# Attention scores of both half heads issued as pairs, with a softmax by chunks of keys

## The chip, the cores and the metric

The kernel runs on one core of a Trainium2 chip. Its time is the device time in microseconds (us) of one execution, as the median of several runs. The engines are named as in the profile: PE multiplies matrices (PEld loads its weights), DVE and ACT work on vectors, POOL adds and issues gathers, SP issues the other transfers.

## What is computed

The reference is one layer of a diffusion backbone over 1024 latent tokens and 256 context tokens of width 1024: modulated norm, one input projection, retention beside differential attention, an output projection with a gated residual, then an expert retrieval (PEER) with another gated residual. The change touches only the attention:

```python
def diff_softmax_attend(q, k, v, lam):
    s = jnp.einsum('bhpqd,bhpkd->bhpqk', q, k).astype(jnp.float32) * (DIFF_D ** -0.5)
    p = jax.nn.softmax(s, axis=-1)
    a = (p[:, :, 0] - lam * p[:, :, 1]).astype(v.dtype)
    return jnp.einsum('bhqk,bhke->bhqe', a, v)
```

There are 4 heads, each of two half heads (index p) of 64 columns. Each half has its own softmax over 1280 keys (1024 latent, 256 context); the second, times lambda, is subtracted from the first. In the expert retrieval each token picks 16 of 16384 experts for each of 8 retrieval heads by two short lists of 128 keys, and sums their outputs.

## The kernel before, in words

**The stages.** Tokens go in 8 blocks of 128. First come the projections of all tokens and the retention. Then `mix` runs over the groups of blocks [0], [4, 5], [6, 7], [3], [1, 2]: `attend` for each block of a group, then the output projection and the norm. `route` follows for each group: query projections, the short lists (`top16`) and the `select` of the experts, on DVE. Blocks 0 to 2 are served by gathers of expert rows (768 of them, each 128 rows of 1024 numbers): POOL issues one, DVE forms a product (`gat<-gat,h2t`) or adds one up (`acc<-gat,act,acc`). Blocks 3 to 7 are served by a dense phase over all experts on PE; ahead of it `gates` writes their weights as a table (`t<-iota`, `o<-iota` on DVE, `o<-o,pt` on ACT). The dense phase needs the gates of block 3, the last; beside its first matmuls the selects of blocks 1 and 2 are still on DVE. The gathers go on beside the dense phase.

**One head of `attend`** (lines 1078 to 1117). For each half p it issues three score matmuls (`mm<-k,t`: 512, 512 and 256 keys) over the 64 partitions of the half, three maxima on DVE, the maximum of the three and its scaling (`m<-m`), then three exponentials on ACT with their sums. When both halves are there, DVE forms the factor `rs`; ACT scales the second half by it (`h<-h,rs`, `u<-u,rs`), and DVE (odd heads) or POOL (even heads, `EC`) adds it to the first (`h<-h`, `u<-u,u`). PE transposes the result in blocks of 128 (`mm<-ident,h`), ACT copies it out, and PE multiplies it with the values (`mm<-v,aT`, `mm<-v,u`).

**What sets the order.** Every operation is recorded and put in order by a planner (class `Plan`): a list scheduler with one queue an engine, modelled costs, priorities, and buffers as limited resources (PSUM is the tag `mm`, 8 banks). `weave` spreads the recorded parts over spans of a common priority (`QSPAN`, `ASPAN`, `HSPAN` and so on), `HOLD` keeps gathers back for a stretch, `PACES` sets their rhythm. Operations inside `with nc.unit()` stay together. Each engine then works through its own list in order. All instructions are issued from one line, so the profile shows line 563 for all; they are told apart by tile names.

Of the kernel before, what the change touches and what calls it, by code (L numbers as in the profile page):

```python
# [30 lines left out]
HOLD = [1000, 1600]  # L31
# [6 lines left out]
QSPAN = [[-0.2, 0.475], [0.1, 1], [-0.05, 1.309], [-0.35, 1.05], [0.15, 0.9]]  # L38
# [3 lines left out]
LSPAN = [[0.479, 1.05], [0.565, 1.218], [0.436, 1.3], [0.05, 0.85]]  # L42
G2SPAN = [0.182, 0.991]
VL, CL, EC, XE = 'D', 'D', 'PD', 'PPPPPPPP'
POFF, PACES = 40, [[0, 3.6], [200, 3.0], [300, 1.17], [700, 1.18], [1100, 1.9]]
# [8 lines left out]
HSPAN = [[-0.25, 0.85], [0.05, 0.796], [0.2, 1.538]]  # L54
# [92 lines left out]
class Plan:  # L147
# [118 lines left out]
    def cost(self, eng, meth, a, k, outs, vs):  # L266
# [303 lines left out]
def layer(tc, I, out, dbg=None):  # L570
# [3 lines left out]
    with sp as S, pp as P, dp as DR:  # L574
        bufs = {"mm": 8, "h": 8, "k": 5, "rv": 4, "b": 4, "v": 5, "sel": 3, "wst": 4, "gat": 4, "fin": 2,  "u1": 3, "u2": 2, "u3": 2,
                "o": 1, "vi": 2, "egb": 3, "pt": 2, "m4": 4, "s1": 2, "act": 2,  "gsum": 2, "rs": 2, "ssum": 2}
# [15 lines left out]
        def ps(shape):  # L592
            return nc.tile(shape, F32, "mm")
# [288 lines left out]
        def qk(kb, pm, which, h0):  # L882
# [185 lines left out]
        def attend(b, res):  # L1068
# [9 lines left out]
            for h in range(H):  # L1078
                nm = sb([128, 2, 4], "m4")
                ssum = sb([128, 2, 4], "ssum")  # L1080
                pl, pc = [], []
                for p in range(2):
                    r = slice(p * 64, (p + 1) * 64)
                    sc3 = [ps([128, 512]), ps([128, 512]), ps([128, 256])]
                    rhs = [KTl[h][r, 0:512], KTl[h][r, 512:1024], KTc[r, h, :]]
                    for i in range(3):
                        nc.tensor.matmul(sc3[i], QT[r, h, :], rhs[i], start=True, stop=True)
                        nc.vector.reduce_max(out=nm[:, p, i:i + 1], in_=sc3[i], axis=AX.X)
                    nc.vector.reduce_max(out=nm[:, p, 3:4], in_=nm[:, p, 0:3], axis=AX.X)
                    nc.vector.tensor_scalar(nm[:, p, 3:4], nm[:, p, 3:4], -SC, None, op0=OP.mult)  # L1090
                    el = sb([128, SEQ], "h")
                    ec = sb([128, CTX], "u1")
                    dsts = [el[:, 0:512], el[:, 512:1024], ec]
                    for i in range(3):
                        nc.scalar.activation(dsts[i], sc3[i], AF.Exp, scale=SC, bias=nm[:, p, 3:4],
                                             accum_out=ssum[:, p, i:i + 1])
                    pl.append(el)
                    pc.append(ec)
# [479 lines left out]
```

## Time and profile before

| | |
|---|---|
| median of 3 runs | 3464.39 us (3459.51 to 3482.91) |
| the profiled execution | 3468.12 us, its span 3466.0 us |
| busy, share of the span | PE 92%, DVE 79%, ACT 38%, POOL 34% |
| mean granted clock of PE | 0.961 of 2.4 GHz |

Busy shares over the whole span hide the stages. The dense phase begins at about 1580 us; attention lies between 400 and 1400 us. So the profile is read by stretches. A group row names an engine, an operation, what it writes and reads, the shape, the count, then busy time, the mean of one in ns, and the idle time of the engine just before with what ended it. A matmul of 4-byte numbers stands as two instructions, so 128 of 512 columns show as x256.

### The profile page before, as it was taken

How to read it: one execution, taken by the hardware profiler on the slowest of the kernel's cores; microseconds unless marked ns; L12 is line 12 of the kernel's file. 1: busy time of each engine (PE TensorE's matmuls, PEld its weight loads, DVE VectorE, ACT ScalarE, POOL GpSimd, SP SyncE). 2: the span in 40 equal slices, each digit the busy share in tenths (PEclk: the TensorE clock that was granted, in tenths of full speed). 3: DMA queues.
4: the chain of work that ended last, by engine and by line, in shares of the span. 5: the costliest groups of instructions: out<-in, count | busy, mean ns of one | idle time of the engine just before them, and what ended most of it. 6: DMA issues, size and time to landing. Idle time of an engine off the chain costs nothing. (4 is left out here: it accounts for less than half of the span.)

```text
span 3466.0 us, 51310 instructions
## 1 busy us (share of the span) xinstructions
PE 3200.0 (92%) x18240; PEld 2745.9 (79%) x18240; DVE 2724.9 (79%) x5902; ACT 1315.0 (38%) x3466; POOL 1188.9 (34%) x1051
## 2 busy tenths in 40 slices
PE   7999996879889789896999999999999999999998
PEld 4998575556678667785898888888889888888887
DVE  4456447779898977969787888788878887888788
ACT  4342343424348679872332222222222222222221
POOL 0101121554340201201454445354545443445442
PEclk9999998889999789997999999999999999999999
DMA  5222655776574434553888888888888888888886
GB/s 183 98 80 83 195 201 172 247 280 232 170 250 163 168 134 141 183 198 113 298 293 298 292 300 282 273 290 301 289 289 297 300 291 271 289 295 292 289 294 231
DMA packets 314529, 809.67 MB, mean 234 GB/s; under 512 B 29313, under 2 KB 125593, under 8 KB 314274
## 3 DMA queue, kind: packets, MB, share of 16 engines
q1 hardware_dynamic: 203682, 403.70, 34.7%
q0 software_dynamic: 110592, 402.70, 33.9%
q8 instruction: 144, 2.36, 0.3%
q14 instruction: 111, 0.91, 0.1%
HBM read 745.46 MB, written 60.83 MB: 233 GB/s over the span
## 5 line engine op out<-in xcount | busy, mean ns | idle before, releaser
L563 PE MATMUL mm<-k,h 128*128 128x384 f32 (+1 forms) x4096 | 916.7, 310 | 20.7 <-DVE h L563 13.3
L563 PEld LDWEIGHTS mm<-k,h 128*128 128x128 f32 x4096 | 693.2, 188 | 35.1 <-DVE h L563 14.9
L563 POOL DMA_INDIRECT gat<-peer_v,egb x377 | 498.1, 1321 | 598.7 <-DVE acc L563 425.2
L563 PE MATMUL mm<-v,h 128*128 128x384 f32 (+1 forms) x2048 | 629.5, 307 | 0.0
L563 ACT CAST h<-wst 128x512 fp32r<-128x512 f32 (+1 forms) x384 | 287.9, 763 | 873.1 <-PE mm L563 841.6
L563 PE MATMUL mm<-h,rv 128*128 128x512 f32 x2304 | 594.8, 397 | 23.8 <-DVE rv L563 22.5
L563 POOL DMA_INDIRECT gat<-peer_u,egb x360 | 421.5, 1171 | 547.8 <-DVE gat L563 287.5
L563 PEld LDWEIGHTS mm<-h,rv 128*128 128x128 f32 x2304 | 425.7, 189 | 127.1 <-DVE rv L563 30.5
L563 DVE SCALAR_TENSOR_TENSOR acc<-gat,act,acc 128x1024 f32<-128x1024 f32 x375 | 480.4, 1281 | 46.2 <-DMA gat<-peer_v,egb 44.7
L563 DVE SCALAR_TENSOR_TENSOR gat<-gat,h2t 128x1024 f32<-128x1024 f32 x360 | 450.8, 1255 | 52.6 <-DMA gat<-peer_u,egb 52.1
L563 PE MATMUL mm<-h,t 128*128 128x512 f32 (+1 forms) x1600 | 423.0, 394 | 15.4 <-DVE b L563 8.3
L563 DVE TENSOR_TENSOR h<-wst,h 128x512 fp32r<-128x512 f32 (+1 forms) x384 | 328.8, 867 | 134.7 <-issue 102.8
L563 PEld LDWEIGHTS mm<-v,h 128*128 128x128 f32 x2048 | 385.1, 188 | 6.3
L563 PEld LDWEIGHTS mm<-h,t 128*128 128x128 f32 x1600 | 295.2, 190 | 88.9 <-DVE b L563 13.6
L563 PE MATMUL mm<-b,wst 128*128 128x256 f32 (+1 forms) x1280 | 242.1, 346 | 3.3 <-ACT b L563 1.5
L563 POOL TENSOR_TENSOR m<-m,mhalf 128x4 f32<-128x4 f32 (+1 forms) x78 | 74.5, 958 | 479.8 <-DVE m L563 469.7
L563 PEld LDWEIGHTS mm<-b,wst 128*128 128x128 f32 x1280 | 208.7, 197 | 30.1 <-issue 3.5
L563 DVE TENSOR_TENSOR b<-b,mm 128x512 f32<-128x512 f32 x248 | 166.3, 684 | 77.6 <-PE mm L563 77.0
L563 PE MATMUL mm<-t,h 128*128 128x256 f32 x992 | 186.8, 286 | 5.9 <-DVE aT L563 3.5
L563 ACT CAST rv<-aT 128x384 fp32r<-128x384 f32 x128 | 65.8, 514 | 329.1 <-DVE aT L563 315.9
L563 DVE TENSOR_TENSOR t<-iota,pt 128x512 f32<-128x512 f32 x240 | 177.2, 772 | 13.3 <-PE mm L563 13.2
L563 PE MATMUL mm<-k,t 64*128 64x512 f32 (+1 forms) x384 | 167.4, 584 | 13.3 <-ACT h L563 12.7
(234 smaller groups left out, 4876.1 us busy)
## 6 DMA issues: line engine op xcount, KB each, us to landing
wst<-peer_u_cols SPq DMA_DIRECT2D x128, 512.0 KB
wst<-peer_v_halves SPq DMA_DIRECT2D x128, 512.0 KB
wst<-w_query_chunks SPq DMA_DIRECT2D x80, 512.0 KB
h<-Wd SPq DMA_DIRECT2D x64, 512.0 KB
wst<-w_mod_chunks SPq DMA_DIRECT2D x48, 512.0 KB
wst<-w_out_chunks SPq DMA_DIRECT2D x40, 512.0 KB
Wd<-rv SPq DMA_DIRECT2D x40, 512.0 KB
Wd<-gat SPq DMA_DIRECT2D x40, 512.0 KB
```

What stands on the lines that cost most here:

```text
L563: getattr(handles[n.eng], meth)(*[res(v) for v in a], **k)
```

## The change

`attend` issues the scores by chunks of keys: for each chunk the two matmuls of both halves stand in one unit, next to each other. Each chunk takes its own maximum on DVE (negated at once) and its exponential follows with that maximum; the scale of 1/8 now lies in the query's copy. When all six chunks are there, factors `f`, the exponentials of the differences between the row's maximum and the chunks' maxima, bring sums and values to the row's maximum. ACT scales each chunk of the second half by its factor; one multiply-add on DVE (`scalar_tensor_tensor`) scales the chunk of the first half and adds. `EC` is 'D' now: DVE does this for all heads and POOL for none. The planner's cost of a matmul over 64 partitions with 256 columns or more is halved, and some numbers of its table differ.

```diff
-HOLD = [1000, 1600]
+HOLD = [1000, 1550]
...
-QSPAN = [[-0.2, 0.475], [0.1, 1], [-0.05, 1.309], [-0.35, 1.05], [0.15, 0.9]]
+QSPAN = [[0.1, 0.475], [0.1, 1], [-0.05, 1.309], [-0.35, 1.05], [0.15, 0.9]]
...
-LSPAN = [[0.479, 1.05], [0.565, 1.218], [0.436, 1.3], [0.05, 0.85]]
+LSPAN = [[0.479, 1.05], [0.565, 1.218], [0.436, 1.3], [0.2, 0.85]]
...
-VL, CL, EC, XE = 'D', 'D', 'PD', 'PPPPPPPP'
-POFF, PACES = 40, [[0, 3.6], [200, 3.0], [300, 1.17], [700, 1.18], [1100, 1.9]]
+VL, CL, EC, XE = 'D', 'D', 'D', 'PPPPPPPP'
+POFF, PACES = 40, [[0, 3.6], [200, 3.0], [300, 1.17], [700, 1.06], [1100, 1.9]]
...
-HSPAN = [[-0.25, 0.85], [0.05, 0.796], [0.2, 1.538]]
+HSPAN = [[-0.25, 0.8], [0.05, 0.796], [0.2, 1.838]]
...
-            return 4 * max(n, 64) * (0.4 if outs[0].shape[0] == 32 else 1) / 2330.0, 0, None, False
+            return 4 * max(n, 64) * (0.5 if n >= 256 and a[1].shape[0] == 64 else 1) / 2330.0, 0, None, False
...
-                nc.scalar.copy(qs, tp)
+                nc.scalar.activation(qs, tp, AF.Copy, scale=SC)
...
-                pl, pc = [], []
-                for p in range(2):
-                    r = slice(p * 64, (p + 1) * 64)
-                    sc3 = [ps([128, 512]), ps([128, 512]), ps([128, 256])]
-                    rhs = [KTl[h][r, 0:512], KTl[h][r, 512:1024], KTc[r, h, :]]
-                    for i in range(3):
-                        nc.tensor.matmul(sc3[i], QT[r, h, :], rhs[i], start=True, stop=True)
-                        nc.vector.reduce_max(out=nm[:, p, i:i + 1], in_=sc3[i], axis=AX.X)
-                    nc.vector.reduce_max(out=nm[:, p, 3:4], in_=nm[:, p, 0:3], axis=AX.X)
-                    nc.vector.tensor_scalar(nm[:, p, 3:4], nm[:, p, 3:4], -SC, None, op0=OP.mult)
...
-                        nc.scalar.activation(dsts[i], sc3[i], AF.Exp, scale=SC, bias=nm[:, p, 3:4],
...
+                for i in range(3):
+                    s2 = [ps([128, keys[i].free]) for p in range(2)]
+                    with nc.unit():
+                        for p in range(2):
+                            r = slice(p * 64, (p + 1) * 64)
+                            nc.tensor.matmul(s2[p], QT[r, h, :], keys[i][r, :], start=True, stop=True)
+                    for p in range(2):
+                        nc.vector.reduce_max(out=nm[:, p, i:i + 1], in_=s2[p], axis=AX.X, negate=True)
+                        nc.scalar.activation(parts[i][p], s2[p], AF.Exp, bias=nm[:, p, i:i + 1],
                                              accum_out=ssum[:, p, i:i + 1])
...
+                nc.vector.tensor_reduce(out=nm[:, :, 3], in_=nm[:, :, 0:3], axis=AX.X, op=OP.min)
+                nc.vector.tensor_tensor(out=f, in0=nm[:, :, 3:4].to_broadcast([128, 2, 3]), in1=nm[:, :, 0:3],
+                                        op=OP.subtract)
+                nc.scalar.activation(f, f, AF.Exp)
...
+                nc.vector.tensor_tensor(out=ssum[:, :, 0:3], in0=ssum[:, :, 0:3], in1=f, op=OP.mult)
...
-                for e in (pc, pl):
-                    nc.scalar.activation(e[1], e[1], AF.Copy, scale=rs[:, 2:3])
-                    eng(EC, h).tensor_tensor(out=e[0], in0=e[0], in1=e[1], op=OP.add)
+                nc.vector.tensor_scalar(f[:, 1, :], f[:, 1, :], rs[:, 2:3], None, op0=OP.mult)
+                for i in (2, 0, 1):
+                    e0, e1 = parts[i]
+                    nc.scalar.activation(e1, e1, AF.Copy, scale=f[:, 1, i:i + 1])
...
+                        nc.vector.scalar_tensor_tensor(e0, e0, f[:, 0, i:i + 1], e1, op0=OP.mult, op1=OP.add)
```

Three places show what moves. In each, the rows of before stand first and those of the change second.

The first is PE's list at the first attention block (`t_4221` and `t_4208` are its queries, `wst,sc` the modulation's projection; here x2 counts matmuls).

```order
L563 MATMUL mm<-k,t_4221 128x512 x2
L563 MATMUL mm<-k,t_4221 128x256
L563 MATMUL mm<-k,t_4221 128x512
L563 MATMUL mm<-wst,sc 2x256 x16
L563 MATMUL mm<-k,t_4221 128x512
L563 MATMUL mm<-k,t_4221 128x256
L563 MATMUL mm<-k,t_4221 128x512 x2
L563 MATMUL mm<-k,t_4221 128x256
L563 MATMUL mm<-k,t_4221 128x512 x2
L563 MATMUL mm<-k,t_4221 128x256
L563 MATMUL mm<-k,t_4221 128x512
```

```order
L564 MATMUL mm<-k,t_4208 128x512 x4
L564 MATMUL mm<-wst,sc 2x256 x8
L564 MATMUL mm<-k,t_4208 128x256 x2
L564 MATMUL mm<-k,t_4208 128x512 x2
L564 MATMUL mm<-wst,sc 2x256 x8
L564 MATMUL mm<-ident,t_4178 128x128 x4
L564 MATMUL mm<-k,t_4208 128x512 x2
L564 MATMUL mm<-ident,u_4309 128x128 x2
L564 MATMUL mm<-ident,h 128x128 x4
L564 MATMUL mm<-v,u_4361 128x128
```

Before, 512, 512 and 256 keys of one half follow each other, and other work falls between; now equal chunks always come by two, one of each half.

The second is DVE's list at the select of block 0, the first of all: before the end of its last step and what follows, now its third to its sixth step. `sel<-sel 128x800` and its reduction are a select's steps, 8 of each.

```order
L563 TENSOR_REDUCE sel<-sel 128x16
L563 CAST egb<-sel 128x128
L563 TENSOR_REDUCE m_5451<-mm 128x1
L563 TENSOR_REDUCE m_5451<-m_5451 128x1
L563 TENSOR_SCALAR m_5451<-m_5451 128x1
L563 TENSOR_TENSOR m_5572<-m_5572 128x1
L563 TENSOR_SCALAR m_5572<-m_5572 128x1
L563 TENSOR_SCALAR t_5156<-mm,rs 128x128
L563 TENSOR_TENSOR sel<-sel 128x128
L563 TENSOR_REDUCE ssum<-ssum 128x2
L563 RECIPROCAL rs<-ssum 128x2
L563 SCALAR_TENSOR_TENSOR rs<-ssum,rs,nlam 128x1
```

```order
L564 TENSOR_TENSOR sel<-sel 128x800
L564 SCALAR_TENSOR_TENSOR h<-h,ff 128x512
L564 SCALAR_TENSOR_TENSOR u_5841<-u_5841,ff,u_5847 128x256
L564 TENSOR_REDUCE sel<-sel 128x16
L564 TENSOR_REDUCE m_5951<-u_5910 128x4
L564 TENSOR_REDUCE m_5953<-mm 128x1
L564 TENSOR_TENSOR sel<-sel 128x800
L564 TENSOR_SCALAR m_5951<-m_5951 128x4
L564 SCALAR_TENSOR_TENSOR h<-h,ff 128x512
L564 TENSOR_REDUCE sel<-sel 128x16
L564 TENSOR_REDUCE m_5953<-mm 128x1
L564 TENSOR_TENSOR sel<-sel 128x800
```

Before, no operation of the softmax stood between the steps, and the add `h<-h` of the head whose `ssum` and `rs` stand here came another four rows down; now maxima and multiply-adds (`h<-h,ff`) of the softmax, and norms of late queries (`m<-u`), stand between the steps.

The third is DVE's list at the last select (block 2), whose end the first dense results wait for (`rv<-aT,rv` are those).

```order
L563 TENSOR_TENSOR sel<-sel 128x800
L563 TENSOR_REDUCE sel<-sel 128x16
L563 CAST egb<-sel 128x128
L563 TENSOR_TENSOR aT<-aT,h 128x256
L563 TENSOR_TENSOR u_14787<-u_14787,h 128x256
L563 TENSOR_TENSOR aT<-aT,t_14201 128x128
L563 TENSOR_TENSOR rv<-aT,rv 128x384
L563 TENSOR_TENSOR u_14836<-u_14836,h 128x256
```

```order
L564 TENSOR_TENSOR sel<-sel 128x800
L564 SCALAR_TENSOR_TENSOR acc<-gat,act,acc 128x1024 x2
L564 TENSOR_REDUCE sel<-sel 128x16
L564 SCALAR_TENSOR_TENSOR acc<-gat,act,acc 128x1024
L564 TENSOR_TENSOR sel<-sel 128x800
L564 TENSOR_REDUCE sel<-sel 128x16
L564 SCALAR_TENSOR_TENSOR gat,act<-gat,h2t 128x1024
L564 TENSOR_TENSOR sel<-sel 128x800
L564 SCALAR_TENSOR_TENSOR gat,act<-gat,h2t 128x1024
L564 SCALAR_TENSOR_TENSOR acc<-gat,act,acc 128x1024
L564 TENSOR_REDUCE sel<-sel 128x16
L564 SCALAR_TENSOR_TENSOR gat,act<-gat,h2t 128x1024
```

Operations on gathered rows, which came behind this select before, now stand between its last steps.

## Rows read from the trace of the kernel before

**Rows 1.** Stretches: length, busy us of PE, PEld, DVE, ACT, POOL; clock, DMA, GB/s.

```profile
400.00:560.00 160.00, 151.12 (x857) 113.16 (x856) 80.54 (x280) 73.59 (x186) 27.12 (x21) 0.97 0.56 189
560.00:600.00 40.00, 14.15 (x77) 10.42 (x75) 34.94 (x124) 11.90 (x32) 10.93 (x22) 0.67 0.32 102
600.00:800.00 200.00, 168.11 (x717) 119.26 (x715) 151.90 (x343) 71.86 (x166) 100.64 (x82) 0.85 0.77 264
800.00:1000.00 200.00, 178.58 (x836) 139.58 (x836) 188.99 (x609) 70.38 (x174) 86.96 (x89) 0.94 0.60 201
1000.00:1140.00 140.00, 135.72 (x778) 113.69 (x779) 121.92 (x388) 112.87 (x390) 25.31 (x19) 0.96 0.58 201
1240.00:1400.00 160.00, 146.64 (x964) 117.47 (x963) 124.71 (x335) 145.51 (x517) 23.45 (x24) 0.99 0.43 144
1580.00:1640.00 60.00, 31.39 (x198) 30.63 (x196) 57.66 (x214) 12.72 (x21) 13.53 (x32) 0.76 0.24 74
1640.00:3466.00 1826.00, 1783.45 (x9790) 1586.19 (x9790) 1514.36 (x2330) 469.72 (x897) 819.73 (x652) 0.99 0.85 287
```

**Rows 2.** Timeline of PE: start, us, names, form of the first, instructions.

```profile
502.81 1.12 PE L563 MATMUL mm<-k,t 64*128 64x512 f32 x2
...
549.06 1.14 PE L563 MATMUL mm<-k,t 64*128 64x512 f32 x4
...
1027.82 1.98 PE L563 MATMUL mm<-k,t 64*128 64x512 f32 x4
```

**Rows 3.** Groups by form, 400 to 1640: names, count | busy, mean ns | idle before.

```profile
L563 PE MATMUL mm<-k,t 64*128 64x512 f32 x256 | 131.4, 663 | 0.6 <-DVE b L563 0.6
L563 PE MATMUL mm<-k,t 64*128 64x256 f32 x128 | 44.0, 426 | 12.7 <-ACT h L563 12.7
L563 PE MATMUL mm<-v,aT 128*128 128x128 f32 x512 | 72.7, 283 | 0.1
L563 PE MATMUL mm<-ident,h 128*128 128x128 f32 x256 | 44.3, 298 | 31.9 <-DVE h L563 30.6 <-POOL h L563 1.0
```

**Rows 4.** The 512-column scores in 400:560, 560:800, 1000:1140 and 1240:1400, in this order.

```profile
L563 PE MATMUL mm<-k,t 64*128 64x512 f32 x62 | 26.7, 644 | 0.0
...
L563 PE MATMUL mm<-k,t 64*128 64x512 f32 x62 | 36.1, 724 | 0.6 <-DVE b L563 0.6
...
L563 PE MATMUL mm<-k,t 64*128 64x512 f32 x28 | 14.7, 626 | 0.0
...
L563 PE MATMUL mm<-k,t 64*128 64x512 f32 x58 | 30.2, 625 | 0.0
```

**Rows 5.** Waits of PE in 560 to 600: total us, times, longest.

```profile
PE mm L563 <- DVE h L563: 25.8, 1, 25.8
```

**Rows 6.** Groups of DVE and ACT by form, 400 to 1640.

```profile
L563 DVE TENSOR_TENSOR h<-h 128x1024 f32<-128x1024 f32 x16 | 19.5, 1220 | 6.1 <-ACT h L563 5.7
L563 DVE TENSOR_TENSOR u<-u,u 128x256 f32<-128x256 f32 x30 | 12.7, 422 | 1.1 <-ACT u L563 0.6
L563 DVE SCALAR_TENSOR_TENSOR acc<-gat,act,acc 128x1024 f32<-128x1024 f32 x17 | 21.8, 1284 | 0.1
L563 DVE SCALAR_TENSOR_TENSOR gat<-gat,h2t 128x1024 f32<-128x1024 f32 x64 | 89.8, 1410 | 15.3 <-DMA gat<-peer_u,egb 15.3
L563 DVE TENSOR_REDUCE m<-mm 128x1 f32<-128x512 f32 x128 | 86.5, 685 | 32.9 <-PE mm L563 31.5 <-issue 1.2
L563 ACT ACTIVATE h<-h,rs 128x1024 f32<-128x1024 f32 x32 | 36.8, 1150 | 19.0 <-DVE rs L563 18.9
L563 ACT ACTIVATE u<-u,rs 128x256 f32<-128x256 f32 x32 | 16.1, 503 | 1.1 <-DVE m L563 0.7 <-DVE rs L563 0.4
```

**Rows 7.** Timeline of POOL and DVE around 1027 us.

```profile
1026.73 3.41 POOL L563 TENSOR_TENSOR h<-h 128x1024 f32<-128x1024 f32 x1 [7.36 <-ACT h L563]
...
1027.84 3.38 DVE L563 SCALAR_TENSOR_TENSOR gat<-gat,h2t 128x1024 f32<-128x1024 f32 x1
```

**Rows 8.** A piece of the chain that ended last: start, us, what.

```profile
3366.01 9.42 DMA gat<-peer_v,egb
```

More of the change, by code (lines that the diff above doesn't have):

```diff
@@ L575, in layer @@
         bufs = {"mm": 8, "h": 8, "k": 5, "rv": 4, "b": 4, "v": 5, "sel": 3, "wst": 4, "gat": 4, "fin": 2,  "u1": 3, "u2": 2, "u3": 2,
-                "o": 1, "vi": 2, "egb": 3, "pt": 2, "m4": 4, "s1": 2, "act": 2,  "gsum": 2, "rs": 2, "ssum": 2}
+                "o": 1, "vi": 2, "egb": 3, "pt": 2, "m4": 4, "s1": 2, "act": 2,  "gsum": 2, "rs": 2, "ssum": 2, "ff": 3}
         def pools(b):
@@ L1080, in attend @@
                 ssum = sb([128, 2, 4], "ssum")
-                pl, pc = [], []
-                for p in range(2):
-                    r = slice(p * 64, (p + 1) * 64)
-                    sc3 = [ps([128, 512]), ps([128, 512]), ps([128, 256])]
-                    rhs = [KTl[h][r, 0:512], KTl[h][r, 512:1024], KTc[r, h, :]]
-                    for i in range(3):
-                        nc.tensor.matmul(sc3[i], QT[r, h, :], rhs[i], start=True, stop=True)
-                        nc.vector.reduce_max(out=nm[:, p, i:i + 1], in_=sc3[i], axis=AX.X)
-                    nc.vector.reduce_max(out=nm[:, p, 3:4], in_=nm[:, p, 0:3], axis=AX.X)
-                    nc.vector.tensor_scalar(nm[:, p, 3:4], nm[:, p, 3:4], -SC, None, op0=OP.mult)
[L1091 to L1094, printed above, removed]
-                        nc.scalar.activation(dsts[i], sc3[i], AF.Exp, scale=SC, bias=nm[:, p, 3:4],
+                f = sb([128, 2, 3], "ff")
@@ new lines, in attend @@
+                pl = [sb([128, SEQ], "h") for _ in range(2)]
+                pc = [sb([128, CTX], "u1") for _ in range(2)]
+                keys = [KTl[h][:, 0:512], KTl[h][:, 512:1024], KTc[:, h, :]]
+                parts = [[e[:, 0:512] for e in pl], [e[:, 512:1024] for e in pl], pc]
+                for i in range(3):
[7 more added lines that the diff above has]
+                        nc.scalar.activation(parts[i][p], s2[p], AF.Exp, bias=nm[:, p, i:i + 1],
@@ L1096, in attend @@
                                              accum_out=ssum[:, p, i:i + 1])
-                    pl.append(el)
-                    pc.append(ec)
+                nc.vector.tensor_reduce(out=nm[:, :, 3], in_=nm[:, :, 0:3], axis=AX.X, op=OP.min)
+                nc.vector.tensor_tensor(out=f, in0=nm[:, :, 3:4].to_broadcast([128, 2, 3]), in1=nm[:, :, 0:3],
+                                        op=OP.subtract)
+                nc.scalar.activation(f, f, AF.Exp)
                 rs = sb([128, 3], "rs")
+                nc.vector.tensor_tensor(out=ssum[:, :, 0:3], in0=ssum[:, :, 0:3], in1=f, op=OP.mult)
@@ L1102, in attend @@
                 nc.vector.scalar_tensor_tensor(rs[:, 2:3], ssum[:, 0, 3:4], rs[:, 1:2], nlam, op0=OP.mult, op1=OP.mult)
-                for e in (pc, pl):
-                    nc.scalar.activation(e[1], e[1], AF.Copy, scale=rs[:, 2:3])
-                    eng(EC, h).tensor_tensor(out=e[0], in0=e[0], in1=e[1], op=OP.add)
+                nc.vector.tensor_scalar(f[:, 1, :], f[:, 1, :], rs[:, 2:3], None, op0=OP.mult)
+                for i in (2, 0, 1):
+                    e0, e1 = parts[i]
+                    nc.scalar.activation(e1, e1, AF.Copy, scale=f[:, 1, i:i + 1])
+                    if EC[h % len(EC)] == "P":
+                        nc.scalar.activation(e0, e0, AF.Copy, scale=f[:, 0, i:i + 1])
+                        nc.gpsimd.tensor_tensor(out=e0, in0=e0, in1=e1, op=OP.add)
+                    else:
+                        nc.vector.scalar_tensor_tensor(e0, e0, f[:, 0, i:i + 1], e1, op0=OP.mult, op1=OP.add)
                 aTl = sb([128, NB, 128], "aT")
```

## The prediction

> **What bounds the kernel now.** I read four views in this order: busy time by stretches of the span, the groups of equal instructions, the waits of PE, and single pieces of the timeline. The stretches [rows 1] show two different kernels. From 1640 us to the end PE is busy 1783 of 1826 us: this is the dense expert phase, whose code the change does not touch. What comes before it ends when the last select on DVE lets the dense phase run, and there the bound changes hands. PE carries 400 to 560 (151 of 160 us) and 1000 to 1140 (136 of 140). DVE carries 560 to 600 (35 of 40), 800 to 1000 (189 of 200) and 1580 to 1640 (58 of 60). In 600 to 800 neither is full (168 and 152 of 200). In 1240 to 1400 PE and ACT are equally full (147 and 146 of 160). All attention lies between 400 and 1400. So a microsecond saved there is worth one at the end only where its engine carries the stretch; in the dense phase nothing is won or lost, and I take its 1826 us as they are.
>
> **The scores on PE.** A score matmul reads 64 partitions; its two half heads lie in partitions 0 to 63 and 64 to 127. The trace of before already holds both cases, since the planner sometimes put two halves side by side by chance [rows 2]. One 512-column matmul (two instructions) takes 1.12 us. Two (four instructions) take 1.98 us in one place and 1.14 us in the other: there the second is free, which I read as two opposite halves, since only these use different partitions. The change issues every pair as one unit, so every pair should look like the third. Per head before: (131.4 + 44.0) / 32 = 5.48 us [rows 3]. After: two pairs of 512 at 1.14 and one pair of 256 at the price of one, 44.0 / 64 = 0.69, together 2.97 us. That is 46% less, 80 us over 32 heads. Where it falls: the 512-column groups by stretch [rows 4], times 175.4 / 131.4 = 1.335 for the 256-column ones, times 0.46, give 16 us in 400 to 560, 22 in 560 to 800, 9 in 1000 to 1140 and 18 in 1240 to 1400; the other 15 lie where DVE carries, and I count them as nothing there: their cover is DVE's work, and if it shrinks they come free. In 400 to 560 and 1000 to 1140 I take the full 16 and 9. In 560 to 800 I take half, 11, because both engines have gaps. In 1240 to 1400 I take half, 9, because ACT ends as late as PE.
>
> **The stall behind the first select.** PE waits 25.8 us in one piece in 560 to 600 for a DVE result [rows 5]: the add that ends a softmax stands behind the whole select of block 0 on DVE, which works in order. The second place of the order shows it, and that the new order puts the softmax operations between the steps of the select. Counted in the two orders, 47 of the 192 maxima precede that select's last step before, 60 now. These 13 are 13/6 = 2.2 heads; a head gives PE 2.97 us of scores, 1.38 of transposes and 2.27 of products with the values [rows 3], 6.6 us in all, so 14 us of PE's work move into the stall. Bounds: 0, if DVE only shifts the wait, and 25.8. I take 14.
>
> **What DVE gets and loses.** The adds of every second head move from POOL to DVE, and all become multiply-adds with a factor per row. A 1024-wide add takes 1.22 us, a 256-wide one 0.42 us, so 512 columns about 0.69; a scalar operand costs 1.284 - 1.220 = 0.064 us more [rows 6]. A head then takes 2 x 0.75 + 0.49 = 1.99 us, 32 heads 64 us, against 16 x (1.22 + 0.42) = 26 us before: **37 us more**. The four small operations a head that replace the four removed ones (a maximum of three and a scaling for each half) I cost at nothing: same width class. In exchange POOL drops 16 adds of 1024 columns and as many of 256. They slow DVE when they meet it: next to one of them a multiply-add, a kind that takes 1.28 us, took 3.38 [rows 6, 7]. Relief lies between 0 and 16 x 2.1 = 34 us; the gathers' products have a mean of 1.41 here, only a tenth above 1.28 [rows 6], so few meet one, and I take 10. Then gathers: the DVE operations on gathered rows ahead of block 5's select are 70 now, 92 before; ahead of the last attention block 98 and 112; at the end of the last select 105 and 112. At 1.35 us each (between 1.28 and 1.41), 560 to 1000 loses 22 x 1.35 = 30 us of DVE work and 4 of the relief, and gets 16 of the 37 us (108 of the 256 score instructions: 62 in 560 to 800 and the 46 that [rows 4] leave for the stretches not shown): 18 us less. DVE carries only 800 to 1000, so I take half, **9 us gained**. From 1000 on 28 gathers come instead of 20, 11 us more, where PE carries; I charge 4. In the last select (third place of the order) come 7 more gathers, in a stretch that DVE fills: **9 us lost**, in full, since PE stands behind it.
>
> **ACT.** The scaling of 1024 columns (1.15 us) becomes two of 512; with 0.50 for 256 columns [rows 6] one costs 0.72, so 0.29 us more a head. An exponential of six columns is new; nothing so small stands in the rows, so between 0 and the 0.50 of 256 columns, 0.25. Together 0.54 us a head, 17 us; 58 of 256 instructions lie in 1240 to 1400, so 4 us there, which I charge, and nothing elsewhere, where ACT has idle time (72 busy of 200 in 600 to 800 and 70 in 800 to 1000).
>
> Nothing else has a price: the changed numbers of the planner's table act only through the order, whose counts are used above; the scale of 1/8 rides on a copy that is made anyway, the number of transfers and gathers is the same, and each chunk's exponential may now follow its own maximum, which shortens a head's chain on ACT by the second and third maximum (0.69 us each) but shows at the end only through the waits already counted. What covers these is DVE's and ACT's idle time; without it they would cost what the rivals say.
>
> **Sum**: -16 - 14 - 11 - 9 - 9 - 9 + 4 + 9 + 4 = -51 us. The profiled execution took 3468.1 us (span 3466.0), so 3417; it lies 4 us above the median of the three runs, by which it would be 3413. I say **3414 us**.
>
> **A rule against it.** A head's maxima cost DVE four times 0.685 us for the 512-column chunks alone [rows 6], 2.7 us, nearly as long as the 2.97 us that its scores on PE will take. The Trainium skill, "TensorEngine Tiling (Array Packing)", section "PSUM Bottleneck", says that packing speeds up TensorE but not the emptying of PSUM, which may then be the bottleneck. No run here shows it yet; by it my sum would shrink to that of the first rival.
>
> **Rivals.**
> 1. *The emptying carries everything* (0.25). DVE and ACT end as late as now from 560 on: the stall only moves, the halves of 560 to 800 and 1240 to 1400 and the 9 of DVE are lost. Left are -16 - 9 + 4 + 9 + 4 = -8: about 3456 on the median, and anything from 3430 to 3480 belongs here. For it: DVE is fuller than PE in three stretches. Against it: DVE has 48 idle us in 600 to 800, and its work there falls.
> 2. *More than forecast* (0.10). The full 80 us of scores, the full stall of 26 and DVE's 18 come through, less 9 + 4 + 4: 107 us, 3357, and the stretch from there to 3389 belongs here. For it: PE's mean granted clock is 0.67 in 560 to 600 and 0.85 in 600 to 800 [rows 1], so a part of both ran at 1.2 GHz, and with shorter stalls other matmuls may run at 2.4.
> 3. *Slower* (0.07): the in-order DVE. Its place is the last select: the gathers that now stand between its steps are issued by POOL only after its last addition. A gather took 9.4 us to land in the last chain [rows 8], and at 287 GB/s [rows 1] seven of 0.52 MB need 13 us more: if DVE arrives first it stands up to 22 us with the select and the dense phase's splits behind it. With the 37 us of adds unrelieved, ACT's 4 and the 9, less 16 in the first stretch and 19 for 14 gathers, that is 22 + 37 + 4 + 9 - 16 - 19 = +37: 3501. It decides if DVE gets there less than some 10 us after POOL; five steps of 2 us of the select lie between, so it is unlikely.
> 4. *The pairs do not overlap* (0.03): another instruction or a wait for a PSUM buffer falls between the two. Then the terms of the scores are gone and -14 - 9 + 4 + 9 + 4 = -6 remain, 3458. Against it: a pair is one unit of the order, first place.
>
> My forecast, 35 to 75 us gained, has 0.55. About 1% (35 us) is what a measurement of this kernel tells from no change. Faster by over 1%: 0.52 of my own case and 0.10, together 0.62; within 1% 0.31 (0.03 of mine, 0.25, 0.03); slower 0.07. The range for 8 in 10 goes from 3375, which leaves out the far part of rival 2, to 3464, which leaves out rival 3, 4 and the upper end of rival 1.
>
> **What would show it.** The score groups fall from 175 to about 95 us busy, with the same counts. PE's wait of 25.8 us is gone or under 12. The dense phase begins 55 to 65 us earlier, PE's 29 us of idle time at its beginning (now in 1580 to 1640) grow by some 9, and from its end to the end of the span it takes 1826 us within 10. If the scores fall but the dense phase starts less than 20 us earlier, rival 1 holds; if DVE waits for gathers in the last select, rival 3. A dense phase that changed its own length by more than 10 us would make the whole argument wrong, since I found no reason for it.

## The result, and the profile after

The changed kernel takes **3452.14 us** (median of 7 runs, 3444.18 to 3456.01). In the same comparison the kernel before took 3477.2 us (7 runs, 3459.51 to 3482.91), 13 more than the three runs that the prediction started from, so the change is read from the ratio: **0.9942 [0.9924, 0.9961]**, 20 us less (13 to 26). The forecast was 51 less, in a range of 3375 to 3464. The sign was right, and the pairs overlap on PE as forecast; the size was not right: it lies within what was called no change. The profiled execution took 3453.47 us, its span 3451.7, 14.3 below before's.

The stretches after, to be read against [rows 1]; the columns are the same, the last two rows are cut where the dense phase now begins:

```profile
400.00:560.00 160.00, 148.96 (x908) 113.83 (x907) 88.39 (x288) 80.75 (x218) 13.94 (x12) 0.98 0.59 193
560.00:600.00 40.00, 30.42 (x143) 20.83 (x142) 34.67 (x154) 17.83 (x49) 9.18 (x20) 0.87 0.35 116
600.00:800.00 200.00, 164.80 (x824) 125.36 (x823) 165.24 (x430) 78.95 (x194) 89.04 (x71) 0.91 0.76 262
800.00:1000.00 200.00, 162.87 (x817) 134.45 (x817) 191.35 (x577) 84.60 (x239) 76.17 (x83) 0.91 0.63 219
1000.00:1140.00 140.00, 125.07 (x775) 108.99 (x773) 128.20 (x452) 114.32 (x413) 11.92 (x19) 0.95 0.53 180
1240.00:1400.00 160.00, 138.83 (x875) 118.36 (x876) 136.47 (x368) 138.88 (x492) 11.64 (x18) 0.91 0.38 128
1537.00:1605.00 68.00, 32.23 (x201) 31.47 (x199) 65.39 (x222) 13.45 (x23) 23.10 (x39) 0.74 0.30 100
1605.00:3451.70 1846.70, 1788.55 (x9790) 1591.88 (x9790) 1519.50 (x2343) 468.47 (x896) 818.80 (x660) 0.99 0.85 287
```

In 560 to 600 PE is now busy 30 us where it was 14. In 1000 to 1140, where PE was full, DVE is now the fuller engine (128 against 125). And the last row is the surprise: behind the last select the dense phase takes 1847 us, where it took 1826.

PE's timeline and score groups, to be read against [rows 2, 3] (x250 and not x256: a few records are missing from the trace):

```profile
488.24 1.99 PE L564 MATMUL mm<-k,t 64*128 64x512 f32 x8
...
534.59 1.13 PE L564 MATMUL mm<-k,t 64*128 64x512 f32 x4
```

```profile
L564 PE MATMUL mm<-k,t 64*128 64x512 f32 x250 | 74.1, 657 | 12.4 <-ACT h L564 8.4 <-DVE b L564 4.0
L564 PE MATMUL mm<-k,t 64*128 64x256 f32 x128 | 24.7, 450 | 0.8 <-DVE b L564 0.8
```

A pair of 512 columns (four instructions) takes 1.13 us, two pairs 1.99. The groups fall from 175.4 to 98.8 us (forecast: 95); how much of that the packing does at equal order, apart shows below.

PE's waits in 560 to 620 (total, times, longest), against [rows 5], and DVE's and ACT's groups against [rows 6]:

```profile
PE mm L564 <- DVE h L564: 4.3, 2, 2.9
PE mm L564 <- DVE ff L564: 3.8, 1, 3.8
```

```profile
L564 DVE TENSOR_REDUCE m<-mm 128x1 f32<-128x512 f32 x128 | 83.0, 682 | 6.9 <-PE mm L564 6.7
L564 DVE TENSOR_REDUCE m<-mm 128x1 f32<-128x256 f32 x64 | 24.4, 415 | 7.6 <-PE mm L564 7.5
L564 DVE SCALAR_TENSOR_TENSOR h<-h,ff 128x512 f32<-128x512 f32 x64 | 50.0, 797 | 4.4 <-ACT h L564 3.6
L564 DVE SCALAR_TENSOR_TENSOR u<-u,ff,u 128x256 f32<-128x256 f32 x32 | 17.5, 546 | 5.1 <-ACT u L564 5.1
L564 ACT ACTIVATE h<-h,ff 128x512 f32<-128x512 f32 x64 | 44.7, 717 | 13.7 <-DVE ff L564 13.6
L564 ACT ACTIVATE ff<-ff 128x6 f32<-128x6 f32 x32 | 7.0, 220 | 10.4 <-DVE ff L564 10.4
```

The wait of 25.8 us is gone; the longest left there is 3.8. The multiply-adds cost 67.5 us (forecast 64), a scaling on ACT 0.717 (0.72), the new exponential 0.22 (0.25).

The dense phase begins with the first matmul `mm<-k,h` in PE's timeline, of before and of the change:

```profile
1579.63 0.42 PE L563 MATMUL mm<-k,h 128*128 128x384 f32 x1
```

```profile
1537.05 0.42 PE L564 MATMUL mm<-k,h 128*128 128x384 f32 x1
```

It begins 42.6 us earlier (forecast 60). From there to the end it lasts 1886.4 us before and 1914.6 now. A first part of that was forecast: PE's longest wait at its beginning, before (in 1580 to 1660) and now (in 1537 to 1640), is the one for the last select:

```profile
PE mm L563 <- DVE rv L563: 18.2, 1, 18.2
```

```profile
PE mm L564 <- DVE rv L564: 28.0, 3, 25.9
```

At the end, the chain that ended last runs through the last gathers and the buffers of the last outputs; before, 73 us of it were PE's last matmuls (a gather lands in 7.0 us there, [rows 8] had 9.4):

```profile
3404.76 6.99 DMA gat<-peer_v,egb
...
3434.46 4.25 DMA out<-b
...
3442.43 3.43 DMA out<-fin
3445.87 2.22 DMA fin<-x1d
```

### The profile page after: what moved, and what is told of

The parts are those of the page before. It is cut to its first block, busy times and chain, and to the rows that moved or that the text cites. A ratio compares the mean times of both kernels' runs of the same rounds, so it can differ in the third digit from the quotient of the medians.

```text
span 3451.7 us, 51441 instructions
## 1 busy us (share of the span) xinstructions
PE 3153.8 (91%) x18240; PEld 2734.5 (79%) x18240; DVE 2731.3 (79%) x5966; ACT 1321.2 (38%) x3528; POOL 1121.8 (32%) x1019
## 5 line engine op out<-in xcount | busy, mean ns | idle before, releaser
L564 POOL DMA_INDIRECT gat<-peer_v,egb x380 | 485.5, 1278 | 543.2 <-DVE acc L564 391.4
L564 POOL DMA_INDIRECT gat<-peer_u,egb x363 | 433.8, 1195 | 614.0 <-DVE gat L564 372.8
L564 PEld LDWEIGHTS mm<-t,h 128*128 128x128 f32 x992 | 158.5, 193 | 7.0 <-DVE aT L564 3.7
```

What stands on the lines that cost most here:

```text
L564: getattr(handles[n.eng], meth)(*[res(v) for v in a], **k)
```

## The experiments

Two questions were open: what packing, adds and maxima are each worth in the front (all ahead of the first dense matmul), and why the dense phase became longer. In this table of all kernels that ran, the dense phase lasts from its first matmul to the end of the span; its pace is the time from the first matmul of group 24 to that of group 120 (of 128 groups of experts, counted from 0, 32 matmuls `mm<-k,h` each). These are from one profiled execution each; the seven kernels with the changed kernel's front, order and work alike, differ by up to 8 us at its end (1536.9 to 1544.7, mean 1540), so smaller differences there mean nothing by themselves. The ratio is to the kernel before, from 4 to 12 runs. "By the ratios" below means the difference of two ratios times 3475 us; "by the medians" means the difference of two medians.

| kernel | ratio | first dense matmul | pace | dense phase |
|---|---|---|---|---|
| before | 1 | 1579.6 | 1380.9 | 1886.4 |
| changed | 0.9942 [0.9924, 0.9961] | 1537.1 | 1386.2 | 1914.6 |
| apart | 1.0040 [1.0022, 1.0058] | 1571.7 | 1378.8 | 1911.3 |
| adds | 0.9881 [0.9856, 0.9906] | 1523.6 | 1383.7 | 1914.5 |
| maxima | 0.9841 [0.9818, 0.9864] | 1519.8 | 1384.8 | 1917.6 |
| fewer | 0.9894 [0.9872, 0.9915] | 1542.6 | 1380.8 | 1894.9 |
| beforefewer | 0.9980 [0.9965, 0.9996] | 1575.7 | 1382.3 | 1883.2 |
| pairs | 1.0244 [1.0220, 1.0269] | 1617.3 | 1376.1 | 1927.3 |
| qspan | 0.9889 [0.9866, 0.9912] | 1563.9 | 1348.5 | 1867.5 |
| fin | 0.9859 [0.9836, 0.9881] | 1556.8 | 1361.9 | 1860.0 |
| table | 0.9920 [0.9897, 0.9943] | 1555.9 | 1348.2 | 1892.0 |
| nogather | 0.9761 [0.9739, 0.9782] | 1541.7 | 1343.4 | 1852.3 |
| finq | 0.9895 [0.9874, 0.9917] | 1537.9 | 1387.3 | 1897.4 |
| beforefin | 0.9912 [0.9890, 0.9933] | 1582.9 | 1358.4 | 1851.4 |
| graft | 0.9823 [0.9799, 0.9848] | 1541.1 | 1349.1 | 1867.3 |
| regraft | 0.9992 [0.9972, 1.0012] | 1566.4 | 1379.7 | 1903.6 |
| graftfin | 0.9782 [0.9758, 0.9806] | 1536.9 | 1362.0 | 1856.5 |
| swap | 1.0011 [0.9992, 1.0029] | 1537.6 | 1402.9 | 1937.7 |
| beforeswap | 1.0116 [1.0098, 1.0134] | 1582.9 | 1418.9 | 1926.1 |
| gfswap | 0.9821 [0.9799, 0.9842] | 1544.7 | 1361.0 | 1858.0 |

### The front: packing, adds, maxima

These three keep the changed kernel's order on every queue, and change only what an instruction works on.

```diff
 # apart
-                            r = slice(p * 64, (p + 1) * 64)
+                            r = slice(0, 64)
 # adds: the multiply-add's operands cut to 17 columns as it is emitted
-    nc.vector.scalar_tensor_tensor(e0, e0, f[:, 0, i:i + 1], e1, op0=OP.mult, op1=OP.add)
+    nc.vector.scalar_tensor_tensor(e0, e0, f[:, 0, i:i + 1], e1, op0=OP.mult, op1=OP.add, cols=17)
 # maxima: the maximum reads 32 columns
-    nc.vector.reduce_max(out=nm[:, p, i:i + 1], in_=s2[p], axis=AX.X, negate=True)
+    nc.vector.reduce_max(out=nm[:, p, i:i + 1], in_=s2[p], axis=AX.X, negate=True, cols=32)
```

**apart.** 

> The changed kernel in its own order of instructions, but both matmuls of a pair read partitions 0 to 63, so they should not overlap (the second half's scores are then those of the first); PE gets back some 75 us of score work (100 us busy become 175). Theory A (after the packing DVE carries 930 to 1200 and 1500 to 1600, so a good part of what PE saves is not passed on): 25 to 50 us slower than the changed kernel's 3452, that is 3477 to 3502. Theory B (the packing is worth all that it takes from PE, the rest was lost by the new order): 60 us or more slower, over 3512. First rival of the prediction (DVE and ACT carry everything from 560 on): at most 20 us slower.

PE's timeline (the two pairs of 488.24 above) and the score groups of apart:

```profile
495.88 3.70 PE L564 MATMUL mm<-k,t 64*128 64x512 f32 x8
```

```profile
L564 PE MATMUL mm<-k,t 64*128 64x512 f32 x255 | 125.9, 618 | 9.8 <-ACT h L564 8.4 <-DVE b L564 1.4
L564 PE MATMUL mm<-k,t 64*128 64x256 f32 x128 | 37.2, 410 | 1.3 <-DVE b L564 1.3
```

Same instructions, same order: two pairs take 3.70 us instead of 1.99 when both halves read the same partitions. PE gets back 163.1 - 98.8 = 64 us, of which 34.6 arrive at the first dense matmul and 34 at the end (1.0040 against 0.9942). Theory A holds: about half is passed on. The other half becomes waits in small pieces: from 400 us to the first dense matmul PE works 1025 us and stands idle 147 in apart, and works 966 and stands idle 172 in the changed kernel (before: 1018 and 161). Without the packing the rest of the change makes the kernel 0.4% slower than before.

**adds** and **maxima.** 

> The changed kernel in its own order, but the 96 multiply-adds that join the two halves work on 17 columns instead of 512 or 256 (the rest of the first half is left unscaled and unjoined). DVE loses 67 - 96 x 0.16 = 52 us of work. Theory A (DVE carries the stretches behind 930): the dense phase starts 20 to 40 us earlier and the end comes 15 to 40 us earlier than 3452. Theory B: PE carries, less than 10 us.

> The changed kernel in its own order, but each of the 192 maxima reads 32 columns of its PSUM bank instead of 512 or 256 (and the queries are scaled by a hundredth of what they were, so that the exponentials stay finite). DVE loses 107 - 192 x 0.15 = 78 us of work that empties PSUM. Theory A: dense phase 30 to 55 us earlier. First rival of the prediction (the emptying of the scores carries everything): 60 us or more. Theory B: less than 10 us.

DVE's groups, of adds and then of maxima:

```profile
L564 DVE SCALAR_TENSOR_TENSOR h<-h,ff 128x17 f32<-128x17 f32 x64 | 15.2, 239 | 12.2 <-ACT h L564 11.6
L564 DVE SCALAR_TENSOR_TENSOR u<-u,ff,u 128x17 f32<-128x17 f32 x32 | 9.9, 310 | 7.2 <-ACT u L564 7.0 <-issue 0.2
```

```profile
L564 DVE TENSOR_REDUCE m<-mm 128x1 f32<-128x32 f32 x190 | 28.1, 184 | 30.9 <-PE mm L564 30.4 <-issue 0.2
```

adds takes 67.5 - 25.1 = 42 us from DVE and gains 13.5 us at the first dense matmul; at the end it gains 21 by the ratios and 14 by the medians. maxima takes 79 us and gains 17.3 there; at the end it gains 35 by the ratios and 28 by the medians (its profiled execution, 3439 us, is the slowest of its five runs, 3413 to 3439). So DVE passes on between a fifth and a half of what it saves, PE half. Neither carries the front alone. In both traces the dense phase begins later than theory A said; the end of adds lies near the lower bound that it gave, 15, or above it. The first rival of the prediction (60 us or more for maxima) is out. The Trainium skill, "TensorEngine Tiling (Array Packing)", section "PSUM Bottleneck", warns that the emptying of PSUM may become the bottleneck after a fourfold speed-up of TensorE. Here the speed-up of the scores is 163 / 99 = 1.65, and three quarters of the maxima taken away bring at most half of their time.

### The dense phase: gathers

**fewer** and **beforefewer** leave out 14 gathers, at the place where the changed kernel is behind, and the first 14 of before's dense phase.

```diff
+ DROP = range(98, 112)      # beforefewer: range(112, 126)
+                    if "drop" in k:        # a dropped step: its DMA and DVE operation are not emitted
+                        [self.nc.vector.memset(res(v), 0.0) for v in k["drop"] if v is not None]
+                        continue
```

> The changed kernel in its own order, but the 14 gathers with numbers 98 to 111 and their operations on DVE are left out (their experts are missing from the sums). The kernel before had 112 gathers done when its dense phase began, the changed one 98. Theory C (the dense phase pays for gathers that it gets: PE and DVE share it, so 14 more lengthen it): 15 to 25 us faster than 3452, of which up to 9 in the last select. Theory D (the dense phase became longer by the chance of the new order at its end): up to 9 us faster, all of it in the last select, and the time from the first dense matmul behind the select to the end stays at 1847.

> The kernel before in its own order, without the 14 gathers with numbers 112 to 125 and their operations on DVE (their experts are missing from the sums): the first 14 that its dense phase carries. If a dense phase pays for every gather that it gets, whatever the order (theory C), this is 9 to 16 us faster than before: the changed kernel without 14 gathers gained 12 us behind its last select, 0.86 each. If only the changed order pays for them (theory D), within 4 us of before.

fewer is 17 us faster than the changed kernel by the ratios (14.2 by the spans). In its trace the last select ends 5.5 + 2.1 = 7.6 us closer to the first dense matmul, and the end another 12. That is theory C for the changed order. But beforefewer gains 7 us (0.2%, 1 to 12), between the two theories, and of the 7 in its trace 3.9 lie ahead of the first gather left out. A gather's price in the dense phase depends on the order around it.

What fewer does not give back lies at the end. Behind the first matmul of group 120 before needs 136.8 us, the changed kernel 149.3 and fewer still 148.4; up to there fewer's dense phase is 3 us shorter than before's. The pace, between groups 24 and 120, differs by only 5 us between before and the changed kernel.

**nogather** leaves out all from 112 on (`DROP = range(112, 768)`).

> The changed kernel in its own order, without the gathers 112 to 767 and their operations on DVE (their experts are missing): the dense phase with nothing beside it. In the trace of the changed kernel the first matmuls of its 24th and 120th group of experts are 1386 us apart. Theory I (the dense phase is not PE's alone: PE waits for DVE, whose queue waits for gathers and for buffers that gathers borrow): these become 1350 or less, and the end comes 40 us or more earlier. Theory D2 (PE sets its length, as the prediction took it): 1375 to 1390, and the end comes less than 25 us earlier.

Busy time in 1900 to 3300, columns as in [rows 1], of the changed kernel, then of nogather:

```profile
1900.00:3300.00 1400.00, 1371.37 (x7549) 1222.32 (x7548) 1159.21 (x1797) 355.89 (x682) 633.23 (x510) 1.00 0.86 290
```

```profile
1900.00:3300.00 1400.00, 1400.00 (x7808) 1263.21 (x7807) 598.96 (x1321) 367.45 (x706) 0.00 (x0) 1.00 0.33 102
```

Theory I holds: the pace falls from 1386 to 1343, the end comes 60 us earlier, and PE has no gap left. So PE alone needs 1343 for these 96 groups; the changed kernel's pace stood 43 us above that, before's 38. The run takes away DVE's work and the transfers together (DMA share 0.86 to 0.33), so it does not tell which of them PE stood behind; the grafts below say more. The sign was in [rows 1]: PE is busy 1783 of 1826 us, but its weight loads only 1586. The Trainium skill, "Perfetto Trace Analysis", section "Identifying the Most-Contended Engine", says that a matmul's busy time is a poor measure of how close PE is to its peak, since matmuls are pipelined, and names the weight loads' busy share as one of two better ones. The trace agrees: between these two rows PE's busy time grows by 2.1%, the loads by 3.3%, like the pace (1386.2 / 1343.4 = 1.032).

### One number put back, and other orders

```diff
 # qspan
-QSPAN = [[0.1, 0.475], ...
+QSPAN = [[-0.2, 0.475], ...
 # table: HOLD, QSPAN, LSPAN, PACES and HSPAN as before
 # fin, beforefin: in the changed kernel and in the one before; finq: fin and qspan
-"fin": 2,
+"fin": 4,
```

**qspan.** 

> The changed kernel with one number of the table put back (the queries of block 0 and its select are spread from -0.2 again instead of 0.1), which moves the first select ahead of 12 of the 60 maxima that now precede its end. Theory F (the stall behind the first select was given up for later gathers): PE's wait of some 20 to 26 us in 560 to 600 is back, the first gather comes 20 to 28 us earlier, and at the end the two nearly cancel: 0 to 12 us slower than 3452. Rival: the stall's 25 us are a gain of their own: 15 to 25 us slower.

PE's waits of qspan in 560 to 610:

```profile
PE mm L564 <- DVE wst L564: 22.0, 1, 22.0
```

The stall is back, as theory F had it, and the dense phase begins 26.8 us later. But the first gathered row is worked on at 610.5 us instead of 622.7 (594.9 before), 12 us earlier and not 20 to 28, and only 100 gathers are issued ahead of the dense phase (98 in the changed kernel, 112 before). And the end comes 18 us *earlier*: the dense phase lasts 1867 us. Theory F and its rival both missed, for the same reason as the prediction.

**table**, **fin**, **beforefin** and **finq.** 

> The changed kernel with the five changed lines of numbers (HOLD, QSPAN, LSPAN, PACES, HSPAN) put back to those of before: the code of the change alone. One of the five alone, put back, gave 3433. Theory H (the packing's 34 us come from the code; what the numbers do is a matter of the new order, mostly in the dense phase, and goes either way): 3425 to 3465, faster than before by 10 to 50 us, with a dense phase that does not last what it did in the changed kernel. Rival (the numbers were what made the change faster): 3465 or more, no gain over before.

> The changed kernel with four buffers instead of two for the tag fin, which the last outputs of a gathered block pass through (the planner makes a new order with them). In the changed kernel the chain that ended last goes through these buffers: DVE waits 3.7 and 2.2 us for loads into them in the last 8 us. Theory G (the tail of the changed kernel is bound by them): 4 to 10 us faster than 3452. Rival: the end stays where PE's last group lets it, less than 3 us, and the rest is the new order's doing, either way.

> The kernel before with four fin buffers instead of two, the control for the changed kernel with four (28 us faster than with two). Theory H (another number of buffers draws another order, and that moves the dense phase either way, whatever the scores do): anything from 25 us faster to 15 slower than before, with another length of the dense phase than 1886. Rival (four buffers serve the changed kernel alone, whose tail waits for them): within 5 us of before.

> The changed kernel with four fin buffers and the one number of the table put back, both of which were faster alone (3424 and 3434). If what they changed are separate places (the tail and the pace of the dense phase) they add up: 3395 to 3415. If both only drew a better order of the dense phase, there is little left: 3415 to 3435.

The code of the change with the old numbers is as fast as with the new (0.9920 and 0.9942, intervals overlap), as theory H had it. Its front gains less (1555.9) and its pace is 1348, but it loses the difference at the end: at group 120 it has 64 gathers left to issue, 26 more than the changed kernel. Two more fin buffers gain 28 us in the changed kernel and **31 in the kernel before**, more than the whole change did. Theory G had no such size, and the control's range ended at 25. The control shows that it is no matter of the changed tail; with four buffers in both, the change is worth 18 us (0.9859 against 0.9912), about what it is worth with two. finq shows that the two gains do not add up: 3439.7 us, 5 above the later half of its expectation, with a pace of 1387 again.

**pairs** issues the pairs with the old softmax: each half keeps the maximum of its row, and the exponentials follow after all six score tiles.

> The kernel before with one part of the change alone: the scores are issued by chunks as pairs, but each half keeps the maximum of its row, the adds stay on POOL and DVE in turn, and the table of numbers is that of before but for the cost of a score matmul. Six of the eight PSUM banks are then held from a head's first score to its exponentials. Theory E (the maximum by chunks is what makes the pairs possible, since it frees a bank at once): PE waits for banks, 20 to 90 us slower than before, although the scores' busy time falls to 100 us. Rival: the pairs alone are the gain, and this is 20 to 40 us faster than before.

It is 85 us slower than before, as theory E expected, with scores of 101 us. But the mechanism was not seen: PE's largest waits are for the adds (400 to 1000, total, times, longest), not for banks; the largest of them is

```profile
PE mm L563 <- POOL h L563: 34.7, 4, 30.4
```

Its trace loses 38 us ahead of the first dense matmul and 56 more up to group 8, with 17 operations on gathered rows between the steps of its last select (8 in the changed kernel) and 13 in the select before that. What the maximum by chunks is worth is not settled by it, since the order changed with it.

### Grafts: order against state

graft, regraft and graftfin cut two plans of the same operations at the first dense matmul, and join the front of one to the rest of the other.

```diff
+    front = sch[:end]                      # sch: the order with FRONT's numbers
+    got = {n.key for n in front}
+    sch = front + [by[k] for k in self.tail[0] if k not in got]   # tail: the order with TAIL's
```

> The changed kernel's order on every engine up to its first dense matmul, from there the order of the kernel with one number of the table put back (qspan); the operations are the same. Theory J (the order within the dense phase sets its length): from the first dense matmul to the end 1867 us within 15, as in qspan, instead of 1915, so an end near 1537 + 1867 = 3404, 35 to 60 us faster than the changed kernel. Theory K (what the front leaves behind sets it: the gathers still to do, the buffers held): 1900 to 1925 as in the changed kernel, an end of 3440 to 3460.

> The reverse: the order of qspan up to the first dense matmul, from there that of the changed kernel. Theory J: the dense phase lasts 1915 us within 15, so an end near 1564 + 1915 = 3479, which makes the change no faster than before. Theory K: 1860 to 1885, an end near 3431 as in qspan.

> The changed kernel's order up to its first dense matmul, from there the order of the kernel with four fin buffers (and the four buffers). Theory J: a dense phase of 1860 us within 15, an end near 1537 + 1860 = 3397, faster than all kernels so far. Theory K: 1890 or more, an end of 3425 or later.

Theory J holds in all three. Busy time in 1900 to 3300 of graft, then of regraft:

```profile
1900.00:3300.00 1400.00, 1396.63 (x7773) 1257.15 (x7772) 1197.44 (x1833) 368.88 (x701) 639.39 (x522) 1.00 0.87 298
```

```profile
1900.00:3300.00 1400.00, 1378.77 (x7632) 1232.81 (x7631) 1165.01 (x1808) 357.72 (x688) 642.16 (x513) 1.00 0.86 291
```

Each dense phase keeps the length of the kernel that its order comes from: 1867.3 with qspan's (1867.5 there), 1903.6 with the changed kernel's (1914.6), 1856.5 with fin's (1860.0), whatever front it follows. The end too goes with the order: regraft needs 148.2 us behind group 120, the changed kernel 149.3. With the changed kernel's dense order behind qspan's front the change is worth nothing (0.9992). With fin's dense order behind its own front it gains 76 us (**graftfin: 3397.34 us**, faster than both kernels), 45 of them against before with as many buffers (0.9782 against 0.9912).

The pace of graft, qspan and table, 1348 to 1349, is within 6 us of nogather's, with all gathers beside it (298 GB/s in graft, 290 in the changed kernel). So neither the transfers nor DVE's work on the gathers as such holds the changed kernel at 1386; their order does. Two limits of these grafts: the fronts joined had issued 95 to 100 gathers, so they do not test what 14 more or fewer would do, and no run joins before's dense order to the changed front.

### What in the order? A miss

In the slow orders DVE waits long at the dense phase's 128x1024 split (73 us before, 89 in the changed kernel, 38 to 43 in qspan, fin and graft, in 1900 to 3300), and an add that frees a PSUM bank stands close behind. swap moves those splits behind the adds, on DVE alone; beforeswap does it in the kernel before, gfswap in graftfin.

```diff
+        for n in [n for n in sch if kind(n) == "split"]:
+            i = sch.index(n)
+            near = [j for j in range(i + 1, min(i + 400, len(sch))) if sch[j].eng == "DVE"][:4]
+            to = [j for j in near if kind(sch[j]) == "add" and not any(n.seq in q.deps for q in sch[i:j])]
+            if to:
+                sch.insert(to[-1], sch.pop(i))
```

> The changed kernel, with one thing moved on DVE alone: a 128x1024 split of the dense phase (h<-wst,h) goes behind the last of those adds (b<-b,mm or t<-t,mm) among the next four DVE operations that do not need it (70 of 128 splits then have an add within the next four, 105 in the changed kernel). Theory L (DVE, working in order, waits at the split for a buffer while the adds that free PSUM banks stand behind it, and PE waits for these): the time from the 24th to the 120th group falls from 1386 to 1350 to 1370 us, and the end comes 15 to 40 us earlier than 3452. Rival (something else in the order, the transfers or the gathers): 1380 or more, within 10 us of 3452.

> The kernel before with the same move of its dense splits on DVE (68 of 128 then have an add within the next four). Theory L: 1381 falls to 1350 to 1370 us, 12 to 30 us faster than before, with the scores as they were. Rival: within 8 us of before.

> The kernel graftfin (the changed front, the dense order of four fin buffers) with the same move; only 69 of its splits had an add within the next four, 58 after it. Theory L: little is left, 0 to 12 us faster than graftfin's 3397, since its 1362 lie 19 above the 1343 without gathers. Rival: slower, since a split moved back delays the next group's matmuls.

DVE's waits in 1900 to 3300 of the changed kernel, then of swap:

```profile
DVE h L564 <- issue: 88.6, 22, 8.0
DVE b L564 <- PE mm L564: 51.3, 37, 3.6
```

```profile
DVE b L579 <- PE mm L579: 158.7, 65, 6.5
```

Theory L fell, and so did the rivals of swap and beforeswap, which saw no such loss. The wait at the split is gone, and the wait at the adds tripled: DVE now stands there, with splits and gathers behind it. swap is 24 us slower than the changed kernel, beforeswap 40 slower than before, gfswap 9 to 14 slower than graftfin (by the medians and by the ratios). In nogather, which has no gap on PE, DVE waits even longer at the same split:

```profile
DVE h L564 <- issue: 154.3, 33, 8.7
```

So a long wait at the split does not mean a slow PE. What ends it the profile does not show ("issue"). What it is in a good order that keeps DVE's results ahead of PE stays open.

## Why the prediction was wrong

**The step that failed** is "in the dense phase nothing is won or lost, and I take its 1826 us as they are", and with it "the changed numbers of the planner's table act only through the order, whose counts are used above". I counted the order in the front and took the dense phase as fixed because its code is untouched. Its order is not: the planner draws it anew. It went from 1826 to 1847 us behind the last select, by my own last sentence the sign that the whole argument is wrong. fewer shows 12 of these 21 as the 14 gathers that the front no longer does and that I priced only where they left and in the last select. The rest lies at the end, behind group 120, and goes with the changed kernel's dense order (148 us in fewer and in regraft, 137 before). The grafts show how much an order can do: the same front has 1857 or 1867 us with another. Had the dense phase kept 1886 us from its first matmul but for the 9 of the last select, the profiled gain would have been 34.

**The front was over-sized by 17** (42.6 of 60; by the mean of the traces of equal order, 39). By steps, the packing from apart against the changed kernel, whose orders are equal. In the front, steps of 5 to 8 us are hardly above what single traces of equal order differ by between such points (4 to 5 us); their sum is clear of it:
- *Scores 400 to 560, -16*: apart reaches the first score of the third block attended 14.8 us later. Right.
- *560 to 1000, -11*: 22.4 - 14.8 = 7.6 up to the first gate. *1000 to 1140, -9*: 27.4 - 22.4 = 5.0; DVE had become the fuller engine, and I took the full 9 because PE was full before. *The rest, -9*: 7.2. Together 34.6 of the 45 forecast. The share passed on was forecast well (45 of 80, measured 34.6 of 64); too large was the 80, since at equal order the packing is 64 of the 77 us by which the scores fell.
- *The stall, -14*: the wait in one piece went as a whole. At the third block's first score, 605.0 us before, the changed kernel is 44.7 ahead, of which apart keeps 29.9. But apart keeps only 7.9 at the first dense matmul, where the stall, DVE and ACT together were forecast at -14 - 9 + 4 + 4 = -15. The first select ended 24.5 us later (612.8 for 588.2), the gathers behind it began 27.8 later, and 14 fewer were done. That the stall was paid for with these gathers is not shown: qspan, with the stall, had done only 2 more than the changed kernel. Where the 22 us went stays open.
- *DVE, 9 gained*: adds shows that 42 of the multiply-adds' 67 us cost 13.5 to 21 us; I had let relief and fewer gathers outweigh them. No run prices the relief.
- *The last select, +9*: 7.6 by fewer (from the first dense matmul to the end of the last select 59.4 us, in the changed kernel and the others of its order 67.0 to 67.2); PE's idle time there went from 28.6 to 35.8. Right.

**Rivals.** The first has the right time (3456, 3430 to 3480) for another reason: the dense phase began 42.6 us earlier, not less than 20, and maxima excludes its mechanism. The second, 75 us and more, did not come. Nor did the third: from the first dense matmul to the end of the last select (1537 to 1605) the only wait of DVE that the profile shows is one of 4.2 us, for ACT and no gather. The fourth is refuted by 1.13 us a pair.

**How the number came about**, in the profiled spans: packing -31 (apart against the changed kernel), the rest of the front -8, the last select +8, gathers in the dense phase +12, and +5 that remain and, by fewer, lie at the end, behind group 120: -14.

## What to carry to other kernels

Where a planner orders the whole program, a change anywhere is a new draw of the order everywhere: here a buffer count that nothing in the front needs was worth 31 us, and one number 18. Price a change at equal order (change what an instruction works on, not where it stands), and try its order against others by joining fronts and rests, before its time is put down to its idea. And a stretch that looks full by matmul time is full only if taking the other engines' work away does not shorten it; its weight loads say more. A pace of 1348 with all gathers, against 1343 without any, shows what is left to win or lose in an order.

## What the runs showed of the hardware

Two matmuls of 4-byte numbers and 512 columns that read opposite halves of the partitions overlap almost wholly: a pair takes 1.13 us, and one alone 1.12 [rows 2]; two pairs take 1.99 us, and 3.70 from the same half. A multiply-add of DVE takes 0.80 us with 512 columns and still 0.24 with 17, a maximum 0.68 with 512 and 0.18 with 32.
